# A state-space and attention trunk: new layout of the recurrence tables, new order of three octets, tail written by halves

## The chip, the cores and the metric

The kernel runs on one core of a Trainium2 chip. The metric is the device time of one execution in microseconds, as the median of several runs. The engines are TensorE (PE, with weight loads shown as PEld), VectorE (DVE), ScalarE (ACT), GpSimd (POOL) and SyncE (SP), which only issues transfers. Each engine takes its instructions in the order in which the kernel writes them.

## What is computed

A decoder trunk of two layers over 528 tokens (16 learned ones and 512 real ones) of width 1024, in float32:

```python
h = concat(meta, x)                                   # 528 x 1024
h = h + s5_mixer(rmsnorm(h, norm_mix[0]), ...)        # layer 0
h = h + swiglu_ffn(rmsnorm(h, norm_ffn[0]), ...)
k, v = split(rmsnorm(h, norm_kv) @ w_kv)
h = h + stick_breaking_attention(rmsnorm(h, norm_mix[1]) @ w_q, k, v) @ w_o   # layer 1
h = h + swiglu_ffn(rmsnorm(h, norm_ffn[1]), ...)
out = rmsnorm(h, norm_final)[16:]
```

The mixer has 64 groups of 16 channels. Each group has a complex diagonal state of 64 entries, which runs over the tokens as x[t] = a x[t-1] + b u[t], with y[t] = Re(c x[t]) + d u[t]. Then come GELU, a product with a 1024 x 2048 matrix and a gate.

## The kernel before

The whole kernel is one program with an order written out by hand: the tile framework adds the semaphores, but no planner moves anything. Weight matrices are loaded by SP in tiles of up to 128 x 1024 (`w_load`) and split into a high and a low part (`w_split`, L113 on ACT and L114 on DVE), and each product is three matmuls (L135).

The recurrence is cut into chunks of T = 8 tokens, 66 chunks in all, and into 8 octets of 8 groups. Two groups (g2 = 0 and 1) form a pair, whose states fill 128 partitions; an octet has four pairs (q). For octet `o` the steps are:

- `e_stage`, `e_fin`, `e_trans`: the input matrices `e` are made on DVE (L248 to L266) with two adds on POOL (L262, L267), turned by PE (L279) and copied out of PSUM by ACT (L282). There is one `e` tile, so the next octet's L259 waits until PE has read it.
- `u_stage`: POOL scales the octet's tokens by the first norm's factor `rsu` (L296). `v_mm`: PE makes the chunk inputs `vp` (L291), 16 products of half the array's width.
- `rot`: DVE turns `vp` by the angles in `ct` and `st` (L595 to L599), runs the scan over the chunks (L603), turns back (L607, L608) and writes the states `s` (L613, L614). `dec_stage` copies the decay on ACT.
- `o_stage`: two products on DVE (L560, L561) of the output matrices, staged in PSUM as `sc` by ACT, and the tables `y1`, `y2`, and an add on POOL (L562) give `ot`.
- `r_mm` (L571, L573) makes the direct part, ACT copies it to `rsb` (L575), SP writes it to DRAM (`rd`, L580) and reads it back as a Toeplitz block (`m`, L582).
- `y_mm`: for each of the 8 groups one product of tokens and `m` (L624) and one of states and `ot` (L625), with the real and imaginary parts of a group's state stacked on 128 partitions. ACT copies `yp` out (L627); `z_out` turns it back (L635) and takes the GELU (L638).

The main loop (L690) runs `i` from 0 to 10: octet `i` in `r_mm`, `m_dma` and `rot`, `a = i + 1` in the input steps, `b = i - 1` in `y_mm` and `z_out`. `FILLS` puts steps of the gated product (`glu1`) between them as work for PE. `tables` (L450) makes `ct` and `st` for two octets at a time with three ACT instructions; `tables(1)` to `tables(3)` stand ahead of the loop. PSUM tiles of two banks come from a pool of three (`bank2`) in turn. Before the loop, `square` and `fold` make the sums of squares, `sincos` the sines (ACT), `int_powers` the integer phase tables (POOL) and `rs_chain` the factor `rsu` (DVE), woven by hand with `e_stage(0)` and `q_chain`, which makes the tables `qr` and `qi`.

The tail takes the last 128 output rows of the last feed-forward product in two halves of 256 tokens, because the final norm needs all of them: `half`, `add_sq`, `sums`, `chain` (the inverse root from an integer start and three Newton steps, on DVE), `spread` (PE copies the factor to all partitions) and `scale` (DVE, then an output transfer from SP or ACT). The hooks `h1` and `h2` put the first half's sums and spread at steps 8 and 20 of the 22 steps of the second half.

Of the kernel before, what the change touches and what calls it, by code (L numbers as in the profile page):

```python
# [31 lines left out]
SQB = 6  # L32
# [3 lines left out]
N1F = len(GLU1)  # L36
PAIRS = (6, 0, 4, 1, 3, 2, 5, 7)
# [10 lines left out]
def trunk_kernel(ctx, tc, xu, xn, prm, octp, gvec, c_id, c_rev, c_i16, c_blk, c_mask,  # L48
# [148 lines left out]
    with ExitStack() as s5x:  # L197
# [13 lines left out]
        y1 = s5.tile([128, T + 1, NPAIR, 2], F32, tag="y1", name="y1")  # L211
        y2 = s5.tile([128, T + 1, NPAIR, 2], F32, tag="y2", name="y2")
# [18 lines left out]
        def loads(o):  # L231
            p = io3.tile([128, 704], F32, tag="op", name="op")
            sp.dma_start(out=p, in_=octp[o])
            opd[o], uu[o] = p, h[o].rearrange("p (g c) -> p g c", g=8)
# [4 lines left out]
        def sc_stage(o):  # L239
            sc_ = bank1("sc")  # L240
            act.activation(out=sc_[:, 0:256], in_=opd[o][:, 192:448], func=ACTF.Copy)
            stg[o] = sc_
# [67 lines left out]
        with tc.tile_pool(name="init", bufs=1) as ini:  # L310
# [107 lines left out]
            int_powers(ph, T + 1)  # L418

            pool.tensor_copy(phc[0][:, 1, :], ph[:, T, 0:8])  # L420
            int_powers(phc[0], NCH)
# [76 lines left out]

            def q_chain():
# [23 lines left out]
            v_mm(0)  # L523
            drain(e_stage(1))
            for c0, c1 in ((0, 4), (4, NPAIR)):
                if c0:
                    tables(0)
                for g2 in range(2):
                    a = slice(64 * g2, 64 * g2 + 64)
                    act.activation(out=y1[0:64, :, c0:c1, g2], in_=qr[a, :, c0:c1], func=ACTF.Copy)  # L530
                    act.activation(out=y1[64:128, :, c0:c1, g2], in_=qi[a, :, c0:c1], func=ACTF.Copy, scale=-1.0)
                    act.activation(out=y2[0:64, :, c0:c1, g2], in_=qi[a, :, c0:c1], func=ACTF.Copy, scale=-1.0)
                    act.activation(out=y2[64:128, :, c0:c1, g2], in_=qr[a, :, c0:c1], func=ACTF.Copy, scale=-1.0)
# [6 lines left out]
        stile = [oc.tile([128, 4, 2, NCH + 1], F32, tag=f"s{i}", name=f"s{i}") for i in range(2)]  # L540
# [7 lines left out]
        def o_stage(o):  # L548
# [6 lines left out]
            def yb(y):  # L555
                return y[:, :, 4 * o:4 * o + 4, :].rearrange("p s q e -> p (q e) s").unsqueeze(3).to_broadcast([128, 8, n, CH])
# [3 lines left out]
            dve.tensor_tensor(out=ot, in0=xb(0), in1=yb(y1), op=ALU.mult)  # L560
            dve.tensor_tensor(out=to, in0=xb(1), in1=yb(y2), op=ALU.mult)  # L561
# [22 lines left out]
        def rot(o):  # L584
# [103 lines left out]
        for j in range(1, 4):  # L688
            tables(j)
        for i in range(0, KD + 3):  # L690
# [19 lines left out]
            if ina:  # L710
# [627 lines left out]
```

## Time and profile before

| | |
|---|---|
| time before, median of 3 runs | 1274.44 us (1273.61 to 1275.99) |
| the profiled execution | 1275.69 us, its span on the core 1273.9 us |
| PE busy | 1206.3 us (95%) |
| DVE busy | 710.6 us (56%) |
| ACT busy | 484.7 us (38%) |
| POOL busy | 328.7 us (26%) |
| mean granted clock of TensorE | 0.976 |

Times within the trace count from the start of the span. The shares are means over stages that differ: PE is almost always busy from 159 us on, while the first 159 us and the last 30 us are mixed.

### The profile page before, as it was taken

The numbers are of one execution on the slowest core, as the hardware profiler recorded it, in microseconds if no ns is written. First come the engines' busy times: TensorE is split into PE (matmuls) and PEld (weight loads), VectorE is DVE, ScalarE is ACT, GpSimd is POOL, SyncE is SP. The second block draws the span as 40 slices with busy tenths as digits, with TensorE's granted clock in tenths as the row PEclk, the third lists the DMA queues.
The fourth block names the chain that finished last, engine by engine and source line by source line (L and its number), as shares of the span: only waits on it lengthen the run. The fifth ranks groups of instructions, "written<-read, shape, count | busy, mean of one in ns | idle before, by whom it ended". The sixth has DMA issues, their size and how long they took to land.

```text
span 1273.9 us, 19766 instructions
## 1 busy us (share of the span) xinstructions
PE 1206.3 (95%) x8206; PEld 1101.3 (86%) x8206; DVE 710.6 (56%) x987; ACT 484.7 (38%) x738; POOL 328.7 (26%) x290
## 2 busy tenths in 40 slices
PE   4588899999999999999999999989999999999996
PEld 3578899999999999999989999868888888888886
DVE  8899547643433433433699888985643444442224
ACT  5544434432222222222666667753432232331120
POOL 6444027211011010111254444344311110111110
PEclk8689999999999999999999999989999999999998
DMA  3455523233223322323212211212233333323321
GB/s 98 88 109 116 117 74 113 91 100 100 83 86 98 89 90 90 91 89 94 79 50 67 67 50 51 65 54 81 67 100 99 99 100 99 95 81 101 95 75 67
DMA packets 44918, 110.15 MB, mean 86 GB/s; under 512 B 4765, under 2 KB 17949, under 8 KB 44829
## 3 DMA queue, kind: packets, MB, share of 16 engines
q1 hardware_dynamic: 43024, 107.64, 29.3%
q8 instruction: 64, 1.05, 0.3%
q10 hardware_dynamic: 1805, 1.26, 0.3%
q14 instruction: 25, 0.20, 0.1%
HBM read 106.14 MB, written 2.74 MB: 85 GB/s over the span
## 4 chain that ended last, share of the span: by engine, by line
PE 81%; DVE 11%; ACT 3%; DMA 3%; issue 2%; POOL 0%; DVEq 0%; SPq 0%; ACTq 0%
PE po L135 19%; PE pgu L135 18%; PE pg L135 14%; PE pu L135 10%; PE pj L135 7%; DVE ga L994 2%; PE pj L1098 2%; PE pv L135 2%; DVE wl L114 2%; DMA m<-rd 1%; PE w L1036 1%; PE po L1191 1%; PE pv L1057 1%; PE yp L624 1%; PE yp L625 1%
## 5 line engine op out<-in xcount | busy, mean ns | idle before, releaser
L114 DVE TENSOR_TENSOR wl<-raw,wh 128x1024 fp32r<-128x1024 f32 (+5 forms) x194 | 242.9, 1258 | 224.8 <-ACT wh L113 221.5
L113 ACT ACTIVATE wh<-raw 128x1024 fp32r<-128x1024 f32 (+5 forms) x194 | 189.1, 979 | 247.1 <-PE po L135 120.3
L820 POOL TENSOR_TENSOR s<-s,rstd 128x528 f32<-128x528 f32 (+1 forms) x44 | 57.4, 1305 | 434.7 <-ACT s L819 434.7
L135 PE MATMUL pgu<-xh,wl 128*128 128x512 f32 x352 | 138.6, 394 | 0.2 <-DVE wl L114 0.2
L135 PE MATMUL pgu<-xl,wh 128*128 128x512 f32 x352 | 138.5, 393 | 0.0
L135 PE MATMUL pgu<-xh,wh 128*128 128x512 f32 x352 | 138.3, 393 | 0.0
L135 PE MATMUL po<-hh,wh 128*128 128x264 f32 (+1 forms) x506 | 132.0, 317 | 0.0
L135 PE MATMUL po<-hh,wl 128*128 128x264 f32 (+1 forms) x506 | 131.9, 317 | 0.0
L135 PE MATMUL po<-hl,wh 128*128 128x264 f32 (+1 forms) x506 | 131.8, 317 | 0.0
L135 PE MATMUL pg<-xh,wl 128*128 128x264 f32 x536 | 109.5, 286 | 2.3 <-DVE wl L114 2.3
L135 PE MATMUL pg<-xh,wh 128*128 128x264 f32 x536 | 110.3, 287 | 1.2 <-ACT ysb L627 0.9
L135 PE MATMUL pg<-xl,wh 128*128 128x264 f32 x536 | 108.9, 285 | 0.0
L1007 POOL TENSOR_TENSOR be<-be,ga 128x415 f32<-128x415 f32 (+1 forms) x48 | 58.1, 1210 | 121.7 <-DVE ga L994 107.4
L135 PEld LDWEIGHTS po<-hl,wh 128*128 128x128 f32 x506 | 83.3, 188 | 7.1
L135 PEld LDWEIGHTS po<-hh,wl 128*128 128x128 f32 x506 | 83.1, 187 | 7.2
L135 PEld LDWEIGHTS po<-hh,wh 128*128 128x128 f32 x506 | 83.2, 188 | 7.1
L819 ACT ACTIVATE s<-g 128x528 f32<-128x528 f32 (+1 forms) x44 | 28.1, 639 | 154.0 <-DVE g L818 154.0
L135 PEld LDWEIGHTS pg<-xh,wl 128*128 128x128 f32 x536 | 83.3, 189 | 2.7 <-DVE wl L114 2.7
L135 PEld LDWEIGHTS pg<-xh,wh 128*128 128x128 f32 x536 | 83.5, 189 | 2.4 <-ACT ysb L627 1.6
L135 PEld LDWEIGHTS pg<-xl,wh 128*128 128x128 f32 x536 | 83.0, 188 | 0.0
L165 POOL TENSOR_TENSOR sq<-h 128x528 f32<-128x528 f32 (+1 forms) x27 | 36.8, 1363 | 173.1 <-DVE h L835 94.1
L135 PEld LDWEIGHTS pgu<-xh,wl 128*128 128x128 f32 x352 | 66.1, 188 | 15.6 <-DVE wl L114 0.6
(338 smaller groups left out, 2573.8 us busy)
## 6 DMA issues: line engine op xcount, KB each, us to landing
raw<-in_w_in SPq DMA_DIRECT2D x88, 512.0 KB, 3.5
raw<-in_w_out SPq DMA_DIRECT2D x32, 512.0 KB, 3.7
raw<-in_w_kv SPq DMA_DIRECT2D x16, 512.0 KB, 3.7
raw<-in_w_out SPq DMA_DIRECT2D x16, 384.0 KB, 3.1
m<-rd SPq DMA_DIRECT2D x8, 512.0 KB
raw<-in_w_q SPq DMA_DIRECT2D x8, 512.0 KB, 3.4
raw<-in_w_o SPq DMA_DIRECT2D x8, 512.0 KB, 3.5
op<-in_octp SPq DMA_DIRECT2D x8, 352.0 KB, 6.9
```

The source lines that it names most:

```text
L113: act.activation(out=wh[:, 0:nk, :], in_=r, func=ACTF.Copy)
L114: dve.tensor_tensor(out=wl[:, 0:nk, :], in0=r, in1=wh[:, 0:nk, :], op=ALU.subtract)
L135: pe.matmul(ps[pc][:, 0:n], lhsT=w[:, k, :], rhs=x[kk][:, c0:c0 + n], start=(first and k == 0 and j == 0), stop=(last and k == nk - 1 and ...
L165: e.tensor_tensor(out=sq[:, 0:n], in0=h[k][:, 0:n], in1=h[k][:, 0:n], op=ALU.mult)
L624: pe.matmul(yo, lhsT=u[:, g, :], rhs=m[:, g, :], start=True, stop=False)
L625: pe.matmul(yo, lhsT=s[:, q, g2, 0:NCH], rhs=ot[:, g, 1:, :].rearrange("p s c -> p (s c)"), start=False, stop=True)
L819: act.activation(out=s_, in_=g_, func=ACTF.Silu)
L820: pool.tensor_tensor(out=s_, in0=s_, in1=rstd[:, 0:n], op=ALU.mult)
L994: dve.tensor_tensor_scan(out=ga[:, c0:c1], data0=ga[:, c0:c1], data1=hide[:, m0:m0 + c1 - c0], initial=init, op0=ALU.mult, op1=ALU.max)
L1007: pool.tensor_tensor(out=be[:, 1:n], in0=be[:, 1:n], in1=ga[:, 0:n - 1], op=ALU.mult)
L1036: pe.transpose(wp[0:n, off:off + 128], src(kt, b), ident)
L1098: pe.matmul(ps, lhsT=w[:, k, :], rhs=x[k], start=(k == 0 and j == 0), stop=(k == KD - 1 and j == 2))
```

## The change

**Layout.** The tables `y1` and `y2`, which 16 ACT copies fill with rearranged and negated halves of `qr` and `qi`, become one tile `q3` that holds qr, -qi and -qr for each pair; DVE writes two of them and ACT one. States of the two groups of a pair stay on their own 64 partitions, real and imaginary parts lie behind each other in `s`. `rot` ends with two operations of 128 partitions where it had four of 64. `y_mm` has, for each group, one product of tokens and `m` as before and two products of 64 partitions each (real and imaginary part), with the two groups of a pair written to different PSUM banks. `octp` shrinks from 704 to 576 columns, `sc_stage` repeats a half as it copies.

**Order.** `SQB` goes from 6 to 5, so one more square follows the sines. `int_powers` becomes `int_steps`, and the last three rounds for octets 2 to 7 come after `v_mm(0)`. In the first three rounds of the loop (`LEAD`) `e_trans` and `dec_stage` stand ahead of `y_mm`; in round 0 also ahead of `r_mm`, with `tables(1)` to `tables(3)` behind `r_mm(0)`.

**Tail.** The table for logarithm and exponential is loaded at the start of the tail, and `chain` takes its start from Ln and Exp on ACT and makes one Newton step. The hooks go to steps 4 and 13, and `h2` scales and writes the whole first half. Of the second half, tiles 3 and 5 (`POOLED`) are scaled by the gain on ACT in `h2` and by the factor on POOL at the end, which reads a copy of it in SBUF.

```diff
-SQB = 6
+SQB = 5
+LEAD = 3
+POOLED = (3, 5)
...
-        y1 = s5.tile([128, T + 1, NPAIR, 2], F32, tag="y1", name="y1")
-        y2 = s5.tile([128, T + 1, NPAIR, 2], F32, tag="y2", name="y2")
+        q3 = s5.tile([128, T + 1, KD, 3, 4], F32, tag="q3", name="q3")
...
-            p = io3.tile([128, 704], F32, tag="op", name="op")
+            p = io3.tile([128, 576], F32, tag="op", name="op")
...
-            act.activation(out=sc_[:, 0:256], in_=opd[o][:, 192:448], func=ACTF.Copy)
+            act.activation(out=sc_[:, 0:256].rearrange("p (i e x) -> p i e x", i=2, e=2),
+                           in_=opd[o][:, 192:320].rearrange("p (i x) -> p i x", i=2).unsqueeze(2).to_broadcast([128, 2, 2, 64]), func=ACTF.Copy)
...
-            def int_powers(p, cnt):
+            def int_steps(p, cnt, n=2, stop=1 << 10):
                 w = p.shape[2]
-                n = 2
-                while n < cnt:
+                while n < min(cnt, stop):
...
-                dve.tensor_tensor(out=qr, in0=qr, in1=qt, op=ALU.subtract)
+                dve.tensor_tensor(out=qv(0), in0=q4(qr), in1=q4(qt), op=ALU.subtract)
+                act.activation(out=qv(2), in_=qv(0), func=ACTF.Copy, scale=-1.0)
                 dve.tensor_tensor(out=qt, in0=pr[:, 1], in1=fb(fr), op=ALU.mult)
                 yield
-                dve.tensor_tensor(out=qi, in0=qi, in1=qt, op=ALU.add)
+                dve.scalar_tensor_tensor(out=qv(1), in0=q4(qi), scalar=-1.0, in1=q4(qt), op0=ALU.mult, op1=ALU.subtract)
...
-                int_powers(phx, NCH)
+                int_steps(phx, NCH, 2, 16)
                 e_fin(0)
                 yield from rs_chain()
...
             v_mm(0)
+            int_steps(phx, NCH, 16)
             drain(e_stage(1))
-            for c0, c1 in ((0, 4), (4, NPAIR)):
-                if c0:
-                    tables(0)
-                for g2 in range(2):
-                    a = slice(64 * g2, 64 * g2 + 64)
-                    act.activation(out=y1[0:64, :, c0:c1, g2], in_=qr[a, :, c0:c1], func=ACTF.Copy)
...
+            tables(0)
...
-        stile = [oc.tile([128, 4, 2, NCH + 1], F32, tag=f"s{i}", name=f"s{i}") for i in range(2)]
+        stile = [oc.tile([128, 2, 4, NCH + 1], F32, tag=f"s{i}", name=f"s{i}") for i in range(2)]
...
-            dve.tensor_tensor(out=ot, in0=xb(0), in1=yb(y1), op=ALU.mult)
-            dve.tensor_tensor(out=to, in0=xb(1), in1=yb(y2), op=ALU.mult)
+            dve.tensor_tensor(out=ot, in0=xb(0), in1=yb(0), op=ALU.mult)
+            dve.tensor_tensor(out=to, in0=xb(1), in1=yb(1), op=ALU.mult)
...
-            for g2 in range(2):
-                a = slice(64 * g2, 64 * g2 + 64)
-                dve.tensor_tensor(out=s[0:64, :, g2, 1:], in0=t1[a, 0], in1=t2[a, 1], op=ALU.subtract)
-                dve.tensor_tensor(out=s[64:128, :, g2, 1:], in0=t1[a, 1], in1=t2[a, 0], op=ALU.add)
+            dve.tensor_tensor(out=s[:, 0, :, 1:], in0=t1[:, 0], in1=t2[:, 1], op=ALU.subtract)
+            dve.tensor_tensor(out=s[:, 1, :, 1:], in0=t1[:, 1], in1=t2[:, 0], op=ALU.add)
...
+            def yo(g):
+                return yp[0:NCH, g % 2, 128 * (g // 2):128 * (g // 2) + 128]
+
+            for g in range(8):
+                pe.matmul(yo(g), lhsT=u[:, g, :], rhs=m[:, g, :], start=(g < 2), stop=False)
+            for q in range(4):
+                for e in range(2):
+                    for g2 in range(2):
+                        a = slice(64 * g2, 64 * g2 + 64)
+                        pe.matmul(yo(2 * q + g2), lhsT=s[a, e, q, 0:NCH], rhs=ot[a, 4 * e + q, 1:, :].rearrange("p s c -> p (s c)"),
+                                  start=False, stop=(q == 3 and e == 1))
             for b in range(2):
-                for g in range(4 * b, 4 * b + 4):
-                    q, g2 = divmod(g, 2)
-                    yo = yp[0:NCH, b, 128 * (g % 4):128 * (g % 4) + 128]
-                    pe.matmul(yo, lhsT=u[:, g, :], rhs=m[:, g, :], start=True, stop=False)
-                    pe.matmul(yo, lhsT=s[:, q, g2, 0:NCH], rhs=ot[:, g, 1:, :].rearrange("p s c -> p (s c)"), start=False, stop=True)
...
-        for j in range(1, 4):
-            tables(j)
         for i in range(0, KD + 3):
...
+            if i == 0:
+                e_fin(a)
+                e_trans(a)
+                dec_stage(a)
             if ini_:
                 rsb = r_mm(i)
-            if ina:
+            if i == 0:
+                for j in range(1, 4):
+                    tables(j)
+            elif ina:
                 e_fin(a)
-                if i:
-                    sc_stage(a)
+                sc_stage(a)
+                if i < LEAD:
+                    e_trans(a)
+                    dec_stage(a)
             if inb:
                 y_mm(b)
...
-            if ina:
+            if ina and i >= LEAD:
                 e_trans(a)
                 dec_stage(a)
...
     def tail(bank2, hh, hl):
         d = KD - 1
+        act.preload_act_table_set("natural_log_exp_and_others")
...
-            dve.tensor_scalar(out=tt.bitcast(I32), in0=vv.bitcast(I32), scalar1=1, scalar2=None, op0=ALU.logical_shift_right)
-            dve.tensor_scalar(out=rr.bitcast(I32), in0=tt.bitcast(I32), scalar1=-1.0, scalar2=float(0x5F3759DF), op0=ALU.mult, op1=ALU.add)
-            for _ in range(3):
-                dve.tensor_tensor(out=tt, in0=rr, in1=rr, op=ALU.mult)
...
+            act.activation(out=tt, in_=vv, func=ACTF.Ln)
+            act.activation(out=rr, in_=tt, func=ACTF.Exp, scale=-0.5)
+            dve.tensor_tensor(out=tt, in0=rr, in1=rr, op=ALU.mult)
...
-            dve.scalar_tensor_tensor(out=fo[k][:, cs(c)], in0=h[k][:, cs(c)], scalar=gv[:, G_FIN, k:k + 1], in1=r, op0=ALU.mult, op1=ALU.mult)
+            if c and k in POOLED:
+                pool.tensor_tensor(out=fo[k][:, cs(c)], in0=fo[k][:, cs(c)], in1=r, op=ALU.mult)
+            else:
+                dve.scalar_tensor_tensor(out=fo[k][:, cs(c)], in0=h[k][:, cs(c)], scalar=gv[:, G_FIN, k:k + 1], in1=r, op0=ALU.mult, op1=ALU.mult)
...
         def h2():
-            box["rb"] = spread(0, box["rr"], box["rp"])
+            rb0 = spread(0, box["rr"], box["rp"])
+            for k in range(KD):
+                scale(0, k, rb0)
+            for k in POOLED:
+                act.activation(out=fo[k][:, cs(1)], in_=h[k][:, cs(1)], func=ACTF.Copy, scale=gv[:, G_FIN, k:k + 1])
...
-        half(1, {8: (h1,), 20: (h2,)})
+        half(1, {4: (h1,), 13: (h2,)})
         add_sq(1)
         rp1 = sums(1)
-        for k in range(3):
-            scale(0, k, box["rb"])
         rr1 = chain(1, rp1)
-        for k in range(3, KD):
-            scale(0, k, box["rb"])
         rb1 = spread(1, rr1, rp1)
+        rbs = x_p.tile([128, NREAL], F32, tag="xl3", name="rbs")[:, 0:HN]
+        act.activation(out=rbs, in_=rb1, func=ACTF.Copy)
         for k in range(KD):
-            scale(1, k, rb1)
+            scale(1, k, rbs if k in POOLED else rb1)
```

The host packing follows the layout (`octp` holds the real and imaginary output matrices once per pair, and the input matrices as blocks of a pair).

## Rows read from the trace of the kernel before

**Rows 1.** Busy times by window: stretch, PE, PEld, DVE, ACT, POOL, clock, DMA.
```profile
159.00:1236.00 1077.00, 1064.29 (x6904) 969.91 (x6903) 563.26 (x687) 404.03 (x583) 260.61 (x212) 1.00 0.28 85
```

**Rows 2.** Chain of waits, 31 to 53 us: start, length, what.
```profile
31.63 0.65 ACT pha L452
...
41.31 0.26 ACT rsb L575
...
43.87 8.67 DMA m<-rd
```

**Rows 3.** Timeline, 11 to 62 us: start, length, engine, line, what, wait before it.
```profile
11.79 0.46 DVE L445 TENSOR_TENSOR pr<-mg,cs 128x288 f32<-128x288 f32 x1 [0.68 <-ACT cs L402]
...
20.76 0.44 POOL L409 TENSOR_TENSOR phx<-phx 128x24 int32<-128x24 int32 x1
...
21.54 0.96 DVE L471 TENSOR_TENSOR tt<-rsu 128x66 f32<-128x66 f32 x1
...
22.67 1.76 POOL L411 TENSOR_TENSOR phx<-phx 128x744 int32<-128x744 int32 x1
...
22.80 1.72 DVE L475 SCALAR_TENSOR_TENSOR rsu<-tt,rsu 128x66 f32<-128x66 f32 x1
...
24.69 0.23 POOL L411 TENSOR_TENSOR phx<-phx 128x24 int32<-128x24 int32 x1
...
25.07 0.23 DVE L475 SCALAR_TENSOR_TENSOR rsu<-tt,rsu 128x66 f32<-128x66 f32 x1
...
31.68 2.65 POOL L562 TENSOR_TENSOR ot<-ot,to 128x1152 f32<-128x1152 f32 x1
...
32.44 2.18 DVE L598 TENSOR_TENSOR t<-t,t 128x264 f32<-128x264 f32 x1
...
39.39 1.36 DVE L560 TENSOR_TENSOR ot<-sc,y 128x1152 f32<-128x1152 f32 x1
...
46.52 0.71 DVE L595 TENSOR_TENSOR t<-vp,ct 128x528 f32<-128x528 f32 x1 [0.51 <-PE vp L291]
...
58.93 0.62 DVE L259 TENSOR_TENSOR e<-sb,pr 128x448 f32<-128x448 f32 x1 [2.96 <-PE ep L279]
...
61.07 0.70 DVE L595 TENSOR_TENSOR t<-vp,ct 128x528 f32<-128x528 f32 x1
```

**Rows 4.** All instructions of line 613: shortest, median, longest (ns).
```profile
L613 DVE TENSOR_TENSOR s<-t,t x16: 426/427/429, 37.6 to 143.4; 64x264 f32<-64x264 f32 x16
```

**Rows 5.** Chain of waits, 110 to 124 us.
```profile
110.07 0.22 PE yp L625 x2
...
123.58 0.55 issue
```

**Rows 6.** Timeline of PE, 59 to 62 us.
```profile
59.77 1.15 PE L291 MATMUL vp<-h,et 128*64 128x66 f32 x32
...
60.86 0.65 PE L571 MATMUL rp<-ot,op 128*32 128x128 f32 x6
```

**Rows 7.** Busy times by window, round 4 of the main loop.
```profile
90.80:108.10 17.30, 14.81 (x158) 13.99 (x158) 16.99 (x25) 8.15 (x17) 8.94 (x6) 1.00 0.58 124
```

**Rows 8.** Who waited for whom, PE, 41 to 160 us: total, times, longest.
```profile
PE yp L624 <- DVE t L596: 1.1, 1, 1.1
```

**Rows 9.** Chain of waits in the tail.
```profile
1256.16 4.35 PE po L1191 x36
...
1263.48 0.17 DVE sml L1206
...
1267.77 3.13 DVE fo L1222 x8
```

**Rows 10.** Timeline of the tail.
```profile
1262.15 0.42 ACT L1195 ACTIVATE sq<-h 128x256 f32<-128x256 f32 x1 [8.58 <-DVE h L1194]
...
1265.86 1.22 PE L1218 MATMUL rp<-ident,sml 128*128 128x128 f32 x4 [2.42 <-DVE sml L1212]
```

**Rows 11.** All output transfers issued by ACT: shortest, median, longest (ns).
```profile
L1224 ACTq DMA_DIRECT2D out<-fo x8: 338/338/353, 1262.5 to 1270.5; - x8
```

More of the change, by code (lines that the diff above doesn't have):

```diff
@@ L417, in trunk_kernel @@
                 fold(j)
-            int_powers(ph, T + 1)
+            int_steps(ph, T + 1)
             pool.tensor_copy(phc[0][:, 1, :], ph[:, T, 0:8])
-            int_powers(phc[0], NCH)
+            int_steps(phc[0], NCH)
             for j in range(4, SQB):
@@ L497, in fb, with q4, qv @@
                 return x.unsqueeze(1).to_broadcast([128, T + 1, NPAIR])
+            def q4(t):
+                return t.rearrange("p s (o q) -> p s o q", q=4)
+            def qv(k):
+                return q3[:, :, :, k, :]
             def q_chain():
@@ L619, in y_mm @@
             ysb = oc.tile([NCH, T, 8, CH], F32, tag="ysb", name="ysb")
-            for b in range(2):
-                for g in range(4 * b, 4 * b + 4):
-                    q, g2 = divmod(g, 2)
-                    yo = yp[0:NCH, b, 128 * (g % 4):128 * (g % 4) + 128]
-                    pe.matmul(yo, lhsT=u[:, g, :], rhs=m[:, g, :], start=True, stop=False)
-                    pe.matmul(yo, lhsT=s[:, q, g2, 0:NCH], rhs=ot[:, g, 1:, :].rearrange("p s c -> p (s c)"), start=False, stop=True)
-            for b in range(2):
-                act.activation(out=ysb.rearrange("p t (b g) c -> p b g t c", b=2)[:, b], in_=yp[0:NCH, b].rearrange("p (g t c) -> p g t c", g=4, t=T), func=ACTF.Copy)
+            def yo(g):
[3 more added lines that the diff above has]
+            for q in range(4):
+                for e in range(2):
+                    for g2 in range(2):
+                        a = slice(64 * g2, 64 * g2 + 64)
+                        pe.matmul(yo(2 * q + g2), lhsT=s[a, e, q, 0:NCH], rhs=ot[a, 4 * e + q, 1:, :].rearrange("p s c -> p (s c)"),
+                                  start=False, stop=(q == 3 and e == 1))
+            for b in range(2):
+                act.activation(out=ysb.rearrange("p t (q b) c -> p b q t c", b=2)[:, b], in_=yp[0:NCH, b].rearrange("p (g t c) -> p g t c", g=4, t=T), func=ACTF.Copy)
             ysbs[o] = ysb
@@ L1206, in chain @@
             dve.tensor_scalar(out=vv, in0=rp[:, 0, 0:2], scalar1=1.0 / D, scalar2=EPS, op0=ALU.mult, op1=ALU.add)
[L1207 to L1212 removed]
+            act.activation(out=tt, in_=vv, func=ACTF.Ln)
+            act.activation(out=rr, in_=tt, func=ACTF.Exp, scale=-0.5)
+            dve.tensor_tensor(out=tt, in0=rr, in1=rr, op=ALU.mult)
+            dve.scalar_tensor_tensor(out=tt, in0=tt, scalar=-0.5, in1=vv, op0=ALU.mult, op1=ALU.mult)
+            dve.scalar_tensor_tensor(out=rr, in0=tt, scalar=1.5, in1=rr, op0=ALU.add, op1=ALU.mult)
             return rr
@@ L1276, in _pack @@
     gu = gp(g0)
-    def dup(x, y):
-        return np.concatenate([x.transpose(1, 0, 2), y.transpose(1, 0, 2)], 0)
-    c1, c2, b2 = dup(cr, cr), dup(ci, ci), dup(br, bi)
-    bb = np.zeros((128, NG, 2, CH), f)
-    bb[:, 0::2, 0], bb[:, 1::2, 1] = b2[:, 0::2], b2[:, 1::2]
+    cw = np.stack([gp(cr), gp(ci)], 1)
+    bb = np.zeros((128, NPAIR, 2, 2, CH), f)
+    for g2 in range(2):
+        for e in range(2):
+            bb[64 * g2:64 * g2 + 64, :, e, g2] = bw[64 * g2:64 * g2 + 64, e]
     o["octp"] = c(np.stack([np.concatenate([
         bw[:, :, 4 * k:4 * k + 4].reshape(128, 128), gu[:, 4 * k:4 * k + 4].reshape(128, 64),
-        c1[:, 8 * k:8 * k + 8].reshape(128, 128), c2[:, 8 * k:8 * k + 8].reshape(128, 128),
-        bb[:, 8 * k:8 * k + 8].reshape(128, 256)], 1) for k in range(KD)]))
+        cw[:, :, 4 * k:4 * k + 4].reshape(128, 128), bb[:, 4 * k:4 * k + 4].reshape(128, 256)], 1) for k in range(KD)]))
     vecs = [a["norm_mix"][0], a["norm_ffn"][0], a["norm_kv"], a["norm_mix"][1], a["norm_ffn"][1], a["norm_final"], a["s5_d"][0]]
```

16 lines of the change are left out of this document (5 added, 11 removed).

## The prediction

> **What bounds the kernel now.** I read the views from coarse to fine: windows, the chain of waits in the two stretches that the diff touches, the timeline there, then who waits for whom. Between 159 and 1236 us TensorE (PE) is busy 1064 of 1077 us at full clock [rows 1]; the diff touches nothing there, so that stretch only shifts. What can move is the state-space part up to about 158 us and the tail after 1245 us.
>
> The state-space part has three regimes. Up to 42 us the chain hops between VectorE (DVE), ScalarE (ACT) and GpSimd (POOL). The first octet's result of `r_mm` waits on ACT behind three `tables` calls (31.63 to 41.31), and only then do `rd` and the 8.67 us `m` transfer start, which `y_mm(0)` needs [rows 2]. From 42 to about 109 us DVE sets the pace: in the window from 90.8 to 108.1 it is busy 16.99 of 17.30 us and PE 14.81 [rows 7], and `y_mm(4)` waits 1.1 us for DVE's L596, which frees its PSUM bank [rows 8]. After that the chain runs through PE. A microsecond of DVE work is therefore worth a microsecond up to octet 4 and little later; one of PE work costs little before octet 5 and its full length after it.
>
> A second thing to see in [rows 3] is that DVE and POOL block each other. L475 has 66 elements and takes 0.23 us alone, but 1.72 us while POOL's 1.76 us L411 runs; L598 takes 2.18 us beside POOL's 2.65 us L562. It meets DVE instructions with both inputs in SBUF; L595, with one input in PSUM, took 0.71 and 0.70 us.
>
> **Head, up to the first scale factor.** With SQB 5 the sixth square moves behind the sines. The multiply after them, L445, waits 0.68 us for ACT [rows 3]: gain 0 to 0.7, I take 0.5. `int_steps` leaves its last six POOL instructions (20.76 to 24.92, 4.1 us) for after `u_stage(0)`. They are what stretched L471 (0.96 us, where L475 of the same size takes 0.23 alone) and L475 (1.72), so `rsu` comes 0.73 + 1.49 = 2.2 us sooner. DVE enters `e_stage(1)` 2.7 us earlier. The 16 ACT copies into `y1` and `y2` vanish; one negated ACT copy of 288 elements replaces them, off the path, since ACT then waits for `e_trans(0)` anyway.
>
> **Where the 2.7 us goes.** The 4.1 us of POOL work is not gone: it stands now ahead of the two adds of `e_stage(1)`, `dg`, `u_stage(1)` and the 2.65 us add of `o_stage(0)`. That add ended at 34.33; undisturbed it now ends at 34.33 - 2.7 + 4.1 = 35.7. `rot(0)` falls on this backlog: L598, L599 and two scans alternate with POOL's instructions, which pushes the add to about 37, and L607 waits for it. I estimate `o_stage(1)` (L560) at 39.4, as before [rows 3]. Bounds: the whole 2.7 is kept, or 1 us is lost. I take zero, since each long POOL instruction in [rows 3] held the DVE one until it ended.
>
> **Order of the first three octets.** `e_trans(1)` comes before `r_mm(0)`, so `e_stage(2)` no longer waits for the transposes, nor `e_stage(3)` (2.96 us at 58.93), nor `rot(1)` for `v_mm(1)` (0.51) [rows 3]. `rot(1)` starts at 44.5 instead of 46.52. But POOL's adds for octet 2 now lie under its L598 and L599 (about 2 us), so `o_stage(2)` is only 0.7 us early. `r_mm(0)` waits for the add at 37: its result leaves ACT at 39.7 instead of 41.57, and `m(0)` lands near 50.7 instead of 52.54 [rows 2]. The three tables follow, 9.7 us, so ACT is busy until 49.4. Queued behind them are the copy of `r_mm(1)` (no gain there), `e_fin(2)` and so `e_trans(2)`, on PE from 50.0 to 52.0. `y_mm(0)` runs 52 to 56.6, then come eviction, `zp` and `v_mm(2)`: `rot(2)` at 59.4 instead of 61.07, 1.7 us early. SP's own order is unchanged; the octet loads shrink from 704 to 576 columns and stay hidden.
>
> **Layout, per octet.** Four 64-partition operations of 0.43 us [rows 4], 0.445 with the gap to the next, become two of 128 partitions: 0.89 us of DVE per octet. While DVE sets the pace this adds up: 1.7 at `rot(2)`, 2.3 after it (part of its 0.89 goes to POOL's adds), 3.2 after `rot(3)`, 4.1 after `rot(4)`, which is what `y_mm(4)` sees. In octet 5 PE still waits 0.55 us [rows 5], so the gain tops out at 4.65.
>
> **Price of the layout on PE.** `y_mm` had 16 products of 0.22 us each (two records per product [rows 5]), 3.5 us. It gets 8 of full depth (1.75) and 16 of half depth, in pairs on partitions 0 to 63 and 64 to 127. No row of before shows half-depth pairs. Bounds: they overlap fully (1.75, no change) or not at all (3.5, +1.75 us per octet). The nearest row is `v_mm`: its 16 half-width products of 66 columns start at 59.77 and the next work at 60.86 [rows 6], 1.09 us, where one after the other they would take 16 x 0.22 x 66/128 = 1.82, so they run 1.67 times faster. By that the half-depth products cost 3.5/1.67 = 2.1 and `y_mm` 3.85 us, +0.35. The path carries it in y(4) to y(7): 4.65 - 4 x 0.35 = 3.2 us left when PE takes over for good.
>
> The Trainium skill (TensorE: Matmul & The Clock Gate, Part 3) gives four row tiles 3.07 times the speed of one, 77% of ideal; by that, an estimate, `y_mm` costs +0.5 and the state-space part would gain 2.6. No run here shows it yet.
>
> **Tail.** The inverse root changes from 12 tiny DVE operations, 2.38 us from 1263.48 to the spread at 1265.86 [rows 9, 10], to four on DVE (0.2 apart) and two on ACT; I price the ACT pair at 0.55 with hand-offs: -1.0. The scalings of the first half move into PE's second half, 13 of 22 steps in: nine steps of 0.36 (12 take 4.35 [rows 9]) are 3.2 us of cover for 8 x 0.39 = 3.13. Five of them lay on the path, 1.9 us from 1265.86 to the first of the last eight at 1267.77; they hid the spread (1.22 [rows 10]), which shows now: -0.7. Two of the eight last scalings go to POOL: -0.8. POOL's price for 256 columns lies between 0.23 for 24 and 1.76 for 744 [rows 3], about 0.7 each, beside DVE, after an ACT copy of 0.42. Against it: ACT issues output DMAs (0.34 each [rows 11]) and two prescalings of 0.42 ahead of the last square [rows 10], +0.4; the cover has no room, +0.2. Sum -1.9; bounds -1.0 (the eight last transfers, not DVE, set the end) and -2.5. The sums at step 4 have 1.4 us of PE work before them and need about 1.0 (add and square). The early table load lies under 22 steps of PE work.
>
> **Sum.** 3.2 + 1.9 = 5.1 us. The profiled execution took 1275.69 us (span 1273.9) and would take 1270.6; it was 1.25 above the median, so the median goes from 1274.44 to 1269.3.
>
> **Rivals.**
> 1. The half-depth products run one after the other, and the kernel is slower. For it: products of full depth follow each other at full price [rows 5], and nothing of before has two row halves. Against: `v_mm` overlaps [rows 6]. Price 1.4 us more than I took in y(0) and y(4) to y(7), 7.0; some 0.6 because PE then paces octet 4, and 0.7 where y(7) starts at a low clock: -5.1 + 8.3 = +3.2, 1277.6. It turns the sign where `y_mm` grows by about 1.3 us per octet. The Trainium skill (TensorEngine Tiling (Array Packing), Tiling Modes, Key Properties) says that a change of tiling mode drains TensorE; that works in this direction in every octet, and no run here shows its length.
> 2. POOL's backlog eats the whole reorder. For it: [rows 3]. Then only two DVE-paced savings (1.8) and the 0.55 remain against 4 x 0.35: 0.95 + 1.9, 1271.6.
> 3. DVE wins the contention and the head's 2.7 us survives, of which PE lets about 2 through: 1267.3. Against: the same rows.
> 4. The tail is paced by its transfers: -1.0 instead of -1.9, 1270.2.
>
> **How the numbers follow.** Forecast 0.54, rival 1 0.14, rival 2 0.12, rival 3 0.12, rival 4 0.08. Predicted: 1269.3. Up to 0.2% (2.5 us, about what a measurement of this kernel can tell from no change) means 1271.9 to 1277.0. Forecast, rivals 3 and 4 are faster; rival 2 lies on the edge, half and half; rival 1 on the other edge, mostly slower; a few hundredths of the forecast fall short. Faster 0.74, same 0.14, slower 0.12. The range runs from 1266 (rival 3 with the best tail) to 1275.5 (rival 1 with pairs that overlap a little); without rival 1 it would end at 1272.
>
> **What would show it.** L445 without wait; L471 and L475 at 0.23; octet 1's L560 near 39.4; `r_mm(0)` out of ACT near 39.7; no wait before L259; octet 2's L595 near 59.4; two operations of 0.43 on 128 partitions where L613 and L614 stand; `y_mm` near 3.85 us at full clock; 1.35 us from the last sums to the spread. Wrong would make it `y_mm` above 4.8 us, or `rot(0)` stretched past 40 us.

## The result, and the profile after

The changed kernel takes 1266.97 us (median of 4 runs, 1264.05 to 1268.09), the kernel before 1274.03 in the runs beside it. The medians differ by 7.1 us. The ratio of the runs is 0.9927, 95% interval 0.9912 to 0.9942: 9.3 us (7.4 to 11.2) of 1274. Timed again (e0 below) the medians differ by 9.9 us and the ratio is 0.9919 (0.9904 to 0.9933). The forecast was 5.1 us; the direction was right, and the gain is 1.4 times as large by the first medians and 1.8 times by the ratio. Applied to the 1274.44 us of before, the ratio gives 1265.1 us, just below the 1266 at which the range of the prediction began.

The profiled execution of after took 1268.09 us (span 1266.4), 7.5 us of span less than the one of before. Line numbers have moved by up to five: L445 is now L446, L560 is L561, L562 is L563, L595 to L599 are L596 to L600, L613 and L614 are L612 and L613, `y_mm` stands at L624 and L629.

First the head and the first octets, in the timeline of after (start, length, engine, line, what, wait before it), to be held against [rows 3]:

```profile
11.02 0.40 DVE L446 TENSOR_TENSOR pr<-mg,cs 128x288 f32<-128x288 f32 x1
12.33 0.84 DVE L250 TENSOR_TENSOR sb<-op 128x128 f32<-128x128 f32 x1 [0.22 <-DMA op<-in_octp]
...
21.78 0.23 DVE L476 SCALAR_TENSOR_TENSOR rsu<-tt,rsu 128x66 f32<-128x66 f32 x1
...
29.94 1.19 DVE L599 TENSOR_TENSOR t<-t,t 128x264 f32<-128x264 f32 x1
31.60 4.69 DVE L604 TENSOR_TENSOR_SCAN w<-dec,t 128x264 f32<-128x264 f32 x2
32.72 3.01 POOL L563 TENSOR_TENSOR ot<-ot,to 128x1152 f32<-128x1152 f32 x1
38.32 0.37 ACT L576 ACTIVATE rsb<-rp,gv 128x128 f32<-128x128 f32 x1 [4.88 <-PE rp L574]
38.38 1.35 DVE L561 TENSOR_TENSOR ot<-sc,q 128x1152 f32<-128x1152 f32 x1
...
58.09 0.71 DVE L596 TENSOR_TENSOR t<-vp,ct 128x528 f32<-128x528 f32 x1 [2.15 <-PE vp L293]
```

L446 has no wait, but most of that is lost at once: L250 waits 0.22 us for the octet's load and is stretched to 0.84 beside a GpSimd step. All nine small operations of the inverse root (L472, L474 and L476, three times each) take 0.22 or 0.23 us. Then GpSimd's backlog, which now holds the doubling steps that were moved, falls on `rot(0)`: the two scans, 1.30 us in octet 3, take 4.69. `o_stage(1)` (38.38) is 1.0 us early all the same.

This table follows the gain through the state-space part. The starts are read from the timelines of the two profiled executions; "forecast" is before less the gain that the prediction gave:

| start of | before | forecast | after | gain forecast | gain measured |
|---|---|---|---|---|---|
| `rot(1)` | 46.52 | 44.5 | 43.44 | 2.0 | 3.1 |
| `rot(2)` | 61.07 | 59.4 | 58.09 | 1.7 | 3.0 |
| `rot(3)` | 76.78 | 74.5 | 72.37 | 2.3 | 4.4 |
| `rot(4)` | 91.14 | 87.9 | 85.67 | 3.2 | 5.5 |
| `y_mm(4)` | 109.20 | 105.1 | 102.65 | 4.1 | 6.55 |
| `y_mm(5)` | 124.13 | 119.5 | 117.12 | 4.65 | 7.0 |

Where did the extra gain per octet come from? The timeline of octet 3 on VectorE, before:

```profile
78.12 0.43 DVE L598 TENSOR_TENSOR t<-t,t 128x264 f32<-128x264 f32 x1
78.48 0.42 DVE L599 TENSOR_TENSOR t<-t,t 128x264 f32<-128x264 f32 x1
78.82 0.70 DVE L644 TENSOR_TENSOR xl<-zf,xh 128x528 fp32r<-128x528 f32 x1
...
82.13 0.43 DVE L613 TENSOR_TENSOR s<-t,t 64x264 f32<-64x264 f32 x1
82.58 0.43 DVE L614 TENSOR_TENSOR s<-t,t 64x264 f32<-64x264 f32 x1
83.03 0.43 DVE L613 TENSOR_TENSOR s<-t,t 64x264 f32<-64x264 f32 x1
83.47 0.43 DVE L614 TENSOR_TENSOR s<-t,t 64x264 f32<-64x264 f32 x1
83.94 1.36 DVE L560 TENSOR_TENSOR ot<-sc,y 128x1152 f32<-128x1152 f32 x1
```

and after:

```profile
77.72 0.43 DVE L612 TENSOR_TENSOR s<-t,t 128x264 f32<-128x264 f32 x1
78.07 0.43 DVE L613 TENSOR_TENSOR s<-t,t 128x264 f32<-128x264 f32 x1
78.42 1.35 DVE L561 TENSOR_TENSOR ot<-sc,q 128x1152 f32<-128x1152 f32 x1
```

Read the starts, not the lengths. Four half-height operations reach from 82.13 to 83.94, 1.81 us; the two of full height from 77.72 to 78.42, 0.70 us. An operation's record is 0.43 us in both, but full-height ones start every 0.35 us and overlap, as L598 and L599 already did in before. The saving is 1.11 us per octet, not 0.89. Why the half-height ones, each written to the other half of the partitions than the one before it, do not overlap was not tried.

Next the price on TensorE, the timeline of `y_mm(4)` after:

```profile
102.65 1.96 PE L624 MATMUL yp<-m,h 128*66 128x128 f32 x16 [0.81 <-DVE t L597]
104.55 1.97 PE L629 MATMUL yp<-ot,s 64*66 64x128 f32 x32
106.44 1.09 PE L281 MATMUL ep<-ident,e 128*128 128x128 f32 x8
```

From its start to that of the next work `y_mm(4)` takes 3.79 us. The forecast was 3.85, against 3.5 in before.

At `y_mm(7)` the profiled gain shrinks again. The timeline, and a window (its start, end and length, busy times of PE, PEld, DVE, ACT and POOL, then granted clock, DMA share, GB/s), after:

```profile
145.09 3.65 PE L624 MATMUL yp<-m,h 128*66 128x128 f32 x16 [3.81 <-DMA m<-rd]
148.67 3.09 PE L629 MATMUL yp<-ot,s 64*66 64x128 f32 x32
```
```profile
145.00:152.00 7.00, 6.91 (x50) 6.45 (x51) 0.00 (x0) 0.20 (x1) 0.00 (x0) 0.57 0.40 137
```

TensorE idles 3.81 us for `m(7)`; then the granted clock averages 0.57, near the lower of its two levels (1.2 of 2.4 GHz), and `y_mm(7)` takes 6.7 us where the other late octets take 3.9. The output products of the first feed-forward part (FFN; `po`, from 478 us) start 4.45 us early. From 159 to 1236 us TensorE is busy for 1064 us, as in [rows 1]. Even so the stretch did not only shift: the attention stage in it, which no edit touches, took 279.76 us in place of 281.19, for which the last section has the rows. So the profiled pair's 7.5 us are 4.45 ahead of that stage, 1.4 in it and 1.6 in the tail.

Last the tail, timeline of after, beside [rows 9, 10]:

```profile
1255.94 0.91 ACT L1252 ACTIVATE fo<-h,gv 128x256 f32<-128x256 f32 x2 [6.35 <-DVE fo L1237]
1256.75 0.40 ACT L1208 ACTIVATE sq<-h 128x256 f32<-128x256 f32 x1
...
1258.07 0.16 DVE L1219 TENSOR_SCALAR sml<-rp 128x2 f32<-128x2 f32 x1 [1.83 <-PE rp L1214]
...
1259.34 0.71 PE L1230 MATMUL rp<-ident,sml 128*128 128x128 f32 x4 [1.31 <-DVE sml L1224]
1260.09 0.38 ACT L1262 ACTIVATE rbs<-rp 128x256 f32<-128x256 f32 x1 [1.39 <-PE rp L1230]
1260.51 2.44 DVE L1237 SCALAR_TENSOR_TENSOR fo<-h,gv,rp 128x256 f32<-128x256 f32 x6 [1.22 <-ACT rbs L1262]
```

From the last sums to the spread it is 1.27 us (forecast 1.35). But ScalarE's two prescalings (L1252, the gain for the tiles that GpSimd scales) hold the last square, and the first of the last scalings starts only after ScalarE's copy `rbs`. From the start of the last tile to the end of the span the tail takes 27.3 us against 28.9, a gain of 1.6.

### The profile page after: what moved, and what is told of

Read it like the earlier page. It is cut to its first block, busy times and chain, and to the rows that moved or that the text cites. A ratio compares the mean times of both kernels' runs of the same rounds, so it can differ in the third digit from the quotient of the medians.

```text
span 1266.4 us, 19985 instructions
## 1 busy us (share of the span) xinstructions
PE 1205.9 (95%) x8334; PEld 1098.6 (87%) x8334; DVE 700.8 (55%) x953; ACT 483.5 (38%) x731; POOL 330.4 (26%) x292
## 4 chain that ended last, share of the span: by engine, by line
PE 82%; DVE 9%; ACT 2%; DMA 2%; issue 2%; POOL 2%; SPq 0%; DVEq 0%; ACTq 0%; POOLq 0%
PE po L137 19%; PE pgu L137 18%; PE pg L137 14%; PE pu L137 10%; PE pj L137 7%; DVE ga L1006 2%; PE pv L137 2%; PE pj L1110 2%; PE w L1048 1%; DVE wl L116 1%; PE pv L1069 1%; PE po L1204 1%; PE yp L624 1%; PE yp L629 1%; PE z L998 1%
```

## The experiments

Two theories stood against each other. **A**: the gain of both recurrence parts was under-sized; VectorE carries it on octet by octet. **B**: the forecast of 3.2 us for them was right, and the rest is the clock in a stretch that the change does not touch. Ratios are to the kernel before, timed on the same chip; gains in us are worked out as (1 - ratio) x 1275.

**The parts alone.** Each kernel is before with some parts of the diff.

```diff
e1: SQB = 5; int_steps split; LEAD order; tables() later
e2: q3, op of 576, stile [2, 4], o_stage, r_mm, rot, y_mm, host tables
e3: POOLED, Ln/Exp chain, scalings in half 2, rbs
e4: e1 and e2
```

> Only the order of the head and of the first three octets is changed; layout and tail stay as before. Theory A (the reorder's gain survives the contention of VectorE and GpSimd and is carried on by VectorE): rot(1) starts some 2.2 us earlier than before, rot(5) still 2.2, and the kernel is 2.4 us faster. Theory B (the forecast as it stood: GpSimd's backlog eats most of it): rot(2) is 0.8 us early and the kernel 0.8 us faster.

Measured: 0.9983 (0.9973 to 0.9993), 2.2 us. `rot(1)` is 2.6 us early, `rot(2)` 2.7, `rot(5)` 1.9: nearer to A.

> Only the layout of the recurrence's tables and states is changed; order and tail stay as before. Both theories: VectorE gains 0.89 us per octet, so rot(5) starts about 4.4 us earlier; y_mm costs 0.35 us more in y(4) to y(7), which leaves 3.0 us. Theory C (the 16 half-depth products and what they do to the clock eat the gain): within 1 us of before.

Measured: 0.9975 (0.9963 to 0.9988), 3.2 us. But `rot(5)` is only 2.2 us early: `rot(2)` starts 1.15 us later than before, and from there each octet gains 1.1.

> Only the final tile is changed. Theory A: 1.6 us faster, as the trace of the changed kernel has it between the start of the last tile's products and the end of the span. The forecast: 1.9 us. Rival (the last transfers pace the end): 1.0 us.

Measured: 0.9987 (0.9974 to 1.0), 1.7 us, an interval that reaches no change; the trace shows the gain better, 27.15 us for the tail in place of 28.9.

> Layout and order together, tail as before. Theory A (VectorE's gains of both parts add up to octet 6 and only the wait for m(7) and the low clock in y_mm(7) take some back): 4.5 to 5.5 us faster, PE's products with x66 lanes after the state-space part start 4.5 us earlier. Theory B (the forecast as it stood, with the gain capped by PE's waits in octet 5; what the whole change gained beyond it is the clock in a stretch that the change does not touch): 3.2 us faster.

Measured: 0.9933 (0.9922 to 0.9945), 8.5 us (7.0 to 9.9), more than the 3.2 of B and the 4.5 to 5.5 of A. The time alone does not refute B, for it holds the untouched stretch too: of the 7.1 us between the spans of before and e4, 4.2 lie ahead of the attention stage and 2.8 in it. The other profiles do. The four with both parts and the old `FILLS` (after, e0, e4, e7 below) reach that stage at 605.4 to 606.5 us, the two with the recurrence of before (before, e3) at 610.7 and 614.3, so every pair has more than 3.2 us ahead of it, 4.2 to 8.9. And the stage takes 279.9 us on average in the seven profiles with both parts and the old `FILLS` (these and e5, e8, e9), 280.1 in the six without both: by these few profiles its clock helped in single runs, not as a rule. Neither theory had the parts worth more together (8.5) than alone (2.2 + 3.2).

**The changed kernel and three edits of it**, on one chip. e0 is the changed kernel itself.

> The changed kernel itself once more, timed beside the three edits of it that follow, as their base: 7 to 9 us faster than before.

Measured: 1266.37 us, 0.9919.

```diff
-            for q in range(4):
-                for e in range(2):
-                    for g2 in range(2):
+            for g2 in range(2):
+                for q in range(4):
+                    for e in range(2):
```

> The changed kernel with the sixteen half-depth products of y_mm ordered so that all of partitions 0 to 63 come first and those of 64 to 127 after them. If neighbouring products of different halves overlap because they alternate (the forecast's reading), this order takes them at full price: 16 x 0.22 = 3.5 us in place of 1.92, y_mm 5.25 us at full clock, 1.4 more, and the path carries it in y(4) to y(7) at least: 5.5 to 7 us slower than the changed kernel, about level with before. Rival: the overlap does not come from the order; y_mm stays near 3.9 us and the time within 1 us of the changed kernel.

Measured: 1273.58 us, 0.9982, 7.2 us slower than the changed kernel. The timeline of `y_mm(4)`:

```profile
104.83 1.96 PE L624 MATMUL yp<-m,h 128*66 128x128 f32 x16 [0.50 <-DVE t L597]
106.72 3.33 PE L629 MATMUL yp<-ot,s 64*66 64x128 f32 x32
109.98 1.09 PE L281 MATMUL ep<-ident,e 128*128 128x128 f32 x8
```

The half-depth products take 3.26 us from start to next work, where alternating ones took 1.89: 1.72 times as long. The same sixteen products in another order cost most of the gain: rival 1 of the prediction was a real price, and the order written in `y_mm` avoids it. One thing was not separated: products on the two halves also write two PSUM banks, so e5 stops the alternation of banks as well. Banks alone are not enough, since the eight full-depth products of L624 alternate between them too and still take their full price, 1.90 us from their start to L629.

```diff
-FILLS = {..., 7: (2, 3), 8: (2, 4), 9: (2, 5)}
+FILLS = {..., 7: (2, 8), 8: (2, 2), 9: (2, 2)}
```

> The changed kernel with five of the gate's 51 fill steps moved into the idle time of TensorE before y_mm(7) (octet 7's iteration takes 2 and 8 of them, the next two 2 and 2 each). Theory A (the low clock in y_mm(7) comes from the 3.8 us idle wait for m(7) and is paid on the path): five steps of 0.73 us fill the wait, y_mm(7) takes 3.9 us in place of 5.4 to 6.7, and the kernel is 5 to 6.3 us faster than the changed one. Rival (the wait is hidden or the moved steps wait for their weights, or delay m(7) by as much): within 1.5 us of the changed kernel.

Measured: 1262.25 us, 0.9888, 4.1 us faster than the changed kernel, nearer to A's 5 to 6.3 than to the rival's 1.5. Timeline and windows at `y_mm(7)`:

```profile
144.74 1.93 PE L624 MATMUL yp<-m,h 128*66 128x128 f32 x16 [0.48 <-DMA m<-rd]
146.60 1.97 PE L629 MATMUL yp<-ot,s 64*66 64x128 f32 x32
```
```profile
140.00:144.00 4.00, 4.00 (x35) 4.00 (x34) 0.91 (x2) 1.24 (x3) 0.00 (x0) 1.00 1.15 162
144.00:148.40 4.40, 3.92 (x51) 3.49 (x49) 0.00 (x0) 0.00 (x0) 0.00 (x0) 1.00 0.83 305
```

The wait shrinks to 0.48, the clock stays at full, and the `po` products start at 471.4 us, 6.8 us earlier than in the profiled run of after (6.0 earlier than in e0's). At the end less is left, for a reason that comes up under the hardware below.

```diff
-                int_steps(phx, NCH, 2, 16)
+                int_steps(phx, NCH)
 ...
-            int_steps(phx, NCH, 16)
```

> The changed kernel with the eight-element-wide doubling steps of GpSimd not split: all of them run before the scale factor, as in before. Theory A (the split takes GpSimd's work off VectorE's path and its later place costs little): rsu is 2.2 us later, rot(1) some 2 us later, and 1.5 to 2.5 us of the gain are lost. Theory B (what the split gives at rsu is lost again to the backlog ahead of the first adds): within 0.7 us of the changed kernel.

Measured: 1267.86 us, 0.9926 (0.991 to 0.9943), an interval that holds e0's value. The timeline on VectorE:

```profile
30.68 0.70 DVE L595 TENSOR_TENSOR t<-vp,ct 128x528 f32<-128x528 f32 x1
...
34.43 1.29 DVE L603 TENSOR_TENSOR_SCAN w<-dec,t 128x264 f32<-128x264 f32 x2
...
42.88 0.70 DVE L595 TENSOR_TENSOR t<-vp,ct 128x528 f32<-128x528 f32 x1
```

`rot(0)` starts 2.95 us later than in e0 (27.73), `rot(1)` only 0.3 later (42.59): the scans run in 1.29 us again. What the split wins at `rsu` it loses to the backlog.

**Order, tail and a better kernel.** e9 is `LEAD = 1`.

> The changed kernel with LEAD 1: in the second iteration the transposes of octet 2 stand behind y_mm(0) again, as in before; the first iteration keeps its new order. Theory A (the order's main worth is that y_mm(0), which runs at a low clock and costs more in the new layout, no longer stands before octet 2's transposes, and VectorE carries that on): rot(2) starts some 3 to 4.5 us later than in the changed kernel, y_mm(6) still 3 us later, and the kernel is 3 us slower than the changed one. Theory B (the forecast: the order is worth under 1 us): within 1 us of the changed kernel.

Measured: 1268.37 us, 0.9932 (0.9914 to 0.995), an interval that holds e0's value. `rot(2)` comes at 59.15, only 1.0 us later than e0's 58.15. VectorE's wait on the way there, e0 and then e9:

```profile
58.15 0.71 DVE L596 TENSOR_TENSOR t<-vp,ct 128x528 f32<-128x528 f32 x1 [3.05 <-PE vp L293]
```
```profile
57.01 0.62 DVE L261 TENSOR_TENSOR e<-sb,pr 128x448 f32<-128x448 f32 x1 [3.58 <-PE ep L281]
```

In either order VectorE waits for work of TensorE that stands behind `y_mm(0)`: in e0 for `v_mm(2)` at `rot(2)` itself, in e9 for the transposes at the next `e_stage`, after which `rot(2)` follows without a wait. My mechanism for the order's worth falls: taking the transposes from behind `y_mm(0)` moves the wait more than it removes it.

```diff
-            for k in POOLED:              # out of h2, into a new hook at step 1 of the second half
-                act.activation(out=fo[k][:, cs(1)], ...)
-        act.activation(out=rbs, in_=rb1, func=ACTF.Copy)
+        rb2 = banks[0][:, 1, 0:HN]
+        for j in range(2):
+            pe.matmul(rb2[:, 128 * j:128 * j + 128], lhsT=rr1[:, j:j + 1]..., rhs=ident)
+        act.activation(out=rbs, in_=rb2, func=ACTF.Copy)
```

> The changed kernel with two edits of its tail: the two prescalings on ScalarE come before the second half's sums instead of just ahead of the last square, and the copy rbs is taken from a second spread of the factor in another PSUM bank. If both lie on the path, as the trace of the changed kernel has them (square held 0.50 us by the prescalings; the first of the last scalings starts 0.42 us late, behind the copy): 0.9 us faster than the changed kernel from the last sums on. Rival (the last transfers or the longer row of small products take it back): no change, within 0.3 us.

Measured: 1265.32 us, 0.9915: not to be told from the changed kernel by time. e10 has both edits and shows them better:

> The changed kernel with the moved fill steps and with the two edits of the tail. If they add up: 4.1 us (measured for the fills) and 0.9 us faster than the changed kernel, 12 to 14 us faster than before.

Measured: 1261.05 us, 0.988 (0.9862 to 0.9897), 15.3 us faster than before. Timeline of its tail:

```profile
1249.27 0.42 DVE L1207 TENSOR_TENSOR h<-h,po 128x256 f32<-128x256 f32 x1
1249.72 0.42 ACT L1208 ACTIVATE sq<-h 128x256 f32<-128x256 f32 x1 [6.70 <-DVE h L1207]
...
1252.33 0.71 PE L1230 MATMUL rp<-ident,sml 128*128 128x128 f32 x4 [1.31 <-DVE sml L1224]
1253.08 0.48 DVE L1237 SCALAR_TENSOR_TENSOR fo<-h,gv,rp 128x256 f32<-128x256 f32 x1 [0.80 <-PE rp L1230]
```

From the last addition into `h` to the first of the last scalings it is 3.81 us, 4.68 in e0: 0.87 less, as expected.

> The same with LEAD 8: the next octet's transposes always stand ahead of y_mm of the one before. Theory A (up to octet 5 VectorE sets the pace and does not wait for TensorE after rot(2)): within 1 us of the run without it. Rival (VectorE's products of the next octet start earlier in every octet): 1 to 2 us faster.

Measured: 1261.41 us, 0.9885, the number of theory A. Its mechanism is not shown: `rot(5)` starts 1.75 us later than in e10 (102.93 and 101.18), and an attention stage of 278.4 us in place of 279.5 hides most of that.

**What was still open**: why the parts are worth more together, and whether `y_mm(7)`'s wait was brought by the change.

> The kernel before with the same five fill steps moved ahead of y_mm(7), and nothing else. Theory A (the wait for m(7) and the low clock behind it are paid by the kernel before as well): 4 to 5 us faster than before, y_mm(7) near 3.7 us. Theory B (the change brought that wait on the path): under 1.5 us.

Measured: 1270.43 us, 0.9965 (0.9952 to 0.9978), 4.5 us, with `y_mm(7)` in 3.68 us. The kernel before pays for that wait too: theory A, the change did not bring it.

```diff
             act.activation(out=rsb, ...)
+            if o == 1:
+                for _ in range(9):
+                    pe.matmul(rp2[:, 1, 0:128], lhsT=ident, rhs=ident, start=True, stop=True)
```

> The layout alone, and after r_mm(1) nine products of the identity with itself, written to an unused PSUM bank (work that no result needs), so that TensorE is busy just before y_mm(0). Theory A (y_mm(0) at a low clock, 6.45 us, stands on the way to octet 2 and takes back the layout's first savings): y_mm(0) takes 3.9 to 4.5 us, rot(2) starts 2 us earlier than with the layout alone, near 60.2, and the gain grows from 3.2 to about 5 us. Rival (y_mm(0) is not on the path, or the nine products do not raise the clock): rot(2) and the time within 0.7 us of the layout alone.

Measured: 1270.94 us, 0.9965 (0.9951 to 0.9979), 4.5 us. `y_mm(0)` with the layout alone (e2):

```profile
52.51 3.65 PE L622 MATMUL yp<-m,h 128*66 128x128 f32 x16 [4.26 <-DMA m<-rd]
56.09 2.87 PE L627 MATMUL yp<-ot,s 64*66 64x128 f32 x32
```

In e2 TensorE's clock had risen by then and fell again while it waited:

```profile
48.00:51.00 3.00, 0.25 (x5) 0.15 (x2) 2.94 (x6) 0.81 (x3) 0.00 (x0) 1.00 1.13 139
52.00:55.00 3.00, 2.49 (x12) 2.52 (x13) 2.53 (x3) 0.00 (x0) 0.60 (x1) 0.50 0.32 106
```

With the nine products ahead of it (e13):

```profile
48.80 2.27 PE L578 MATMUL rp<-ident 128*128 128x128 f32 x18 [0.51 <-ACT rsb L575]
52.13 1.93 PE L626 MATMUL yp<-m,h 128*66 128x128 f32 x16 [1.06 <-DMA m<-rd]
54.00 1.97 PE L631 MATMUL yp<-ot,s 64*66 64x128 f32 x32
```

The nine products begin with the clock already up (1.00 from 48.8 us on) and fill the wait in which e2's fell. From 52.4 to 55.0 us it is 1.00 in place of 0.50, `y_mm(0)` takes 3.84 us in place of 6.45, and `rot(2)` starts at 59.22 in place of 62.22, more than expected. By `y_mm(6)` only 0.8 of the 3.0 is left: VectorE now waits 1.73 us at 103.96 for ScalarE's half of a weight split, and one operation meets GpSimd (1.12 us at 89.42 in place of 0.43). The place is shown; of its worth in the whole time, the intervals of e2 and e13 overlap.

> The run with moved fills and the two tail edits, and five such products after r_mm(1). Theory A: y_mm(0) 3.9 us in place of 4.7, rot(2) 0.8 us earlier, the kernel 0.8 us faster than without them. Rival: no change, within 0.3 us.

Measured: 1261.46 us, 0.9895 (0.9879 to 0.991): the rival. Here the five products start behind 2.57 us of idle time at a clock of 0.50 and take 2.3 us themselves; they hold up octet 2's transposes and `y_mm(0)` (51.85 in place of 50.27), which takes 4.64 us, 4.69 in e10. `rot(2)` comes 1.5 us later, not earlier.

> The run with moved fills and the two tail edits, with GpSimd's doubling steps not split. The forecast's step (what the split gives at rsu is lost to the backlog): within 0.7 us of the run with the split, rot(0) 2.9 us later but rot(1) level. The other reading (the split is worth 1.5 us, the difference of the medians of the first such run): 1.5 us slower.

Measured: 1259.42 us, 0.9876 (0.9862 to 0.9891), the fastest of all: 15.8 us (13.9 to 17.6) less than before. `rot(0)` is 2.4 us later than in e10, `rot(1)` level (42.97 and 43.19). On this evidence the split is worth nothing.

## Why the prediction was right and wrong

**Head: right in kind.** The wait at L445 went, and its gain was smaller (0.26 us at L261, before's L259) than the 0.5 taken. The inverse root ran at 0.23 us throughout, `rsu` 2.5 us early (2.2 forecast). That the split's 2.7 us then vanish in the backlog was taken from [rows 3] and is right for the time: e8 and e15 show it from the other side. Rival 3 (the head's gain survives) would have given the measured time, by a mechanism that the runs refute.

**The step that failed: the gain on VectorE, 4.1 us at `y_mm(4)`, measured 6.55.** The mechanism held and the term was mis-sized, in three places. (1) "0.89 us of DVE per octet" multiplied lengths; full-height operations overlap, and it is 1.11. (2) I let the backlog push GpSimd's add of octet 0 to about 37. It ended at 35.73, the undisturbed figure of my own text (35.7), since VectorE's scans were held up instead. So `r_mm(0)` left ACT at 38.69, not 39.7, and `y_mm(0)` began at 50.54, not 52; and octet 0's layout saving, which I gave to the contention too, was kept: `o_stage(1)` 1.0 us early. (3) In octet 2 I took 0.3 of 0.89 off for GpSimd's adds; measured was a gain of 1.4 between `rot(2)` and `rot(3)`, more than the layout's own 1.11: a wait of 0.32 us for ScalarE that VectorE had there in before (63.51) is gone too.

With what was measured the forecast's own sum gives 7.0 at `y_mm(5)`, less 4 x 0.3 for `y_mm`, plus 1.6 in the tail: 7.4 us, the lower end of the ratio's interval and close to the 7.1 by which the medians differ. The 2 us up to 9.3 are not traced to a cause; the scatter of `y_mm(7)` and of the attention stage, below, is of that size.

**Order: right in kind.** `rot(1)` gained 3.1 us, 2.0 by the forecast: 1.0 that `o_stage(1)` was early, and 2.1 from the waits of 1.58 us at L259 and 0.51 at L595 in before, which the new order removes. No wait stands before octet 3's L261. But the chain through `m(0)` and `y_mm(0)` sets `rot(2)` in every variant looked at, through the transposes or through `v_mm(2)` (e9). With the layout alone, `y_mm(0)` grows at the low clock and takes back what VectorE had saved until then (e2, e13); with the order alone, a collision at `rot(2)` (1.37 us for L601) takes 0.9. At `rot(5)` the two together are 5.2 to 6.5 us early (e4, e7, e0, after), alone 2.2 and 1.9: a surplus of 1.1 to 2.4, the size of these two losses. Of the 3.1 us of surplus in the timed runs the rest is within the scatter of the three intervals.

**Price on TensorE: right.** 3.79 us against 3.85 forecast, now shown by rows of half-depth pairs. Rival 1's price of 1.4 us per octet was right as well, for the other order of the same products (e5: 1.36). The Trainium skill (TensorE: Matmul & The Clock Gate, Part 3) has four row tiles at 3.07 times the speed of one, 77% of ideal. Two row halves here reach 1.72 of 2, 86%. The Trainium skill's warning of a drain at a change of tiling (TensorEngine Tiling (Array Packing), Tiling Modes, Key Properties) shows in no gap: L629 follows 1.90 us after L624 starts, of which 8 x 0.22 = 1.76 are products, so a drain is at most 0.14 us.

**Where PE takes over: right.** I let TensorE's idle 0.55 us in octet 5 raise the gain from 4.1 to 4.65; it rose from 6.55 to 7.0. That the stretch from 159 us on "only shifts" was wrong: its attention stage alone differs by up to 2.8 us between profiles.

**`y_mm(7)`.** I gave it 0.35 us. Its wait and its clock scatter: the kernel before took 5.34 us from 151.08 in its profile, and 6.63 from 152.85 in e3, which has the same recurrence. One pair of profiles can therefore not give the recurrence's gain; the timed runs of e4 do, 8.5 us (7.0 to 9.9).

**Tail: 1.9 forecast, 1.6 measured.** I had ScalarE's prescalings ahead of the square; what I missed is that VectorE's scalings wait for ScalarE's copy of the same PSUM tile (0.4 us; gone in e10, where the copy reads another bank).

## What to carry to other kernels

Price a row of short instructions by the distance of their starts, not by their recorded lengths: the records overlap, and where one engine sets the pace the error comes once per round. Where two engines hold each other up, ask which of them the next stage waits for: here GpSimd's long add nearly kept its time (3.01 us in place of 2.65) and VectorE paid. And look for the idle wait that stands ahead of a stretch of products: ready work moved into it paid twice, once for the wait and once for the clock after it.

## What the runs showed of the hardware

The attention stage, which no edit touches, takes 278.35 to 281.2 us from its first projection to the FFN's first product in the profiles of these kernels, the kernel before included (281.2). It goes with the granted clock behind a wait of TensorE for VectorE. Windows of before and of e4 in that stage:

```profile
848.00:854.00 6.00, 5.40 (x16) 4.42 (x17) 2.99 (x5) 1.50 (x3) 0.53 (x1) 0.50 0.30 87
```
```profile
844.00:850.00 6.00, 5.59 (x32) 4.86 (x33) 3.21 (x6) 2.53 (x5) 0.35 (x1) 1.00 0.30 89
```

and the instruction before which TensorE waited, first before, then e4:

```profile
848.60 0.90 PE L1036 MATMUL w<-ident,be 128*128 128x128 f32 x3 [3.15 <-DVE wtl L1047]
```
```profile
844.41 0.55 PE L1048 MATMUL w<-ident,be 128*128 128x128 f32 x3 [3.17 <-DVE wtl L1059]
```

Behind the same wait, 3.15 and 3.17 us, the clock stood at 0.50 in one run and at 1.00 in the other: the stage took 281.2 and 278.35 us. In e0 the clock fell 12 us earlier, behind another wait, of 1.99 us (0.50 from 832 to 834 us); TensorE then came later to this one, which shrank to 1.59, and the stage took 278.35 us as well. So a gain of a few us earlier in the program can grow or shrink by 2.8 us here: e6 started this stage 6.0 us ahead of e0 and left it 3.1 ahead. Why the fall comes in one run and not in the next was not tried.

Two things more. Products without use kept a clock that was up (e13: nine of them, 1.00 during and after) and did not lift one that was down (e14: five of them, 0.50 during, and still 0.50 when `y_mm(0)` began). And VectorE's two scans of 264 elements took 4.69 us beside GpSimd's backlog and 1.29 without it.
